# Attention times V on one core: the first unit's load as two halves instead of one transfer

## Chip, cores, metric

One core of one Trainium2 chip. The metric is the device time in microseconds of one execution. "Fast runs" are executions in the chip's normal state.

## The reference

```python
# attn_weights (8, 12, 1024, 1024) float32, v (8, 12, 1024, 64) float32
return np.einsum('bhqs,bhsd->bhqd', attn_weights, v).astype(np.float32)
```

403 MB of attention weights have to be read once and each element is used for 64 products, so the kernel lives from its transfers.

## The kernel before

The work is cut into 48 units. A unit is one load of 128 partitions x 16 rows x 1024, fp32 in memory, cast to bf16 by the DMA, 8 MB read and 4 MB written. Two buffers `abf[0]` and `abf[1]` take the units in turn. PE transposes the 16 rows through four PSUM banks (two bf16 as one fp32 word), VectorE and ScalarE copy each bank out into `at`, PE multiplies with V. The next load into a buffer is issued by GpSimd when the unit in it is transposed. The last two units are loaded in halves, with one semaphore for each second half. (PE is TensorE, the engine for matmuls; a PSUM bank is the buffer that it writes and from which the copies read. A relay by SyncE waits for a load's semaphore and passes it on to PE as `s_half`.)

```python
HALVED = NU - 2                              # NU = 48 units
...
def pe_unit(i, n, loaded, it):
    pe.wait_ge(*loaded)                      # the load (or its first half) has landed
    for g in range(G):                       # 16 rows
        if g == GH:
            pe.wait_ge(s_half, n)            # the second half too: SyncE relays it
        transpose_g(abf[i], g, n)            # g >= 4 waits for the copy of row g - 4
    ...                                      # spread V, transpose back, multiply
...
# VectorE, in program order: V first, then the copies of every unit
nc.vector.wait_ge(s_v0, 16 * 4)
nc.vector.tensor_copy(out=vr..., in_=v32).then_inc(s_vr, 2)
engine(True)
...
# GpSimd
load_attn(0)
load_attn(1)
...
for n in range(NU - 2):
    ...
    pool.wait_ge(s_t[True], (n + 1) * PER_DVE)   # unit n is transposed
    load_attn(n + 2)
    ...                                          # bursts of output stores
...
# SyncE: V's first part by four transfers, then the relays to s_half, then the last stores
```

Of the kernel before, what the change touches and what calls it, by code (L numbers as in the profile page):

```python
# [10 lines left out]
def kernel(  # L11
# [29 lines left out]
    G = Q // VP // 2  # L41
    GH = G // 2
# [5 lines left out]
    NU = 2 * NV  # L48
# [7 lines left out]
    RING = 5  # L56
    NO = 2 * RING

    HALVED = NU - 2

    def slot(q):
        return q % NO
# [20 lines left out]
    with tc.tile_critical(no_gpsimd_drain=True):  # L83
        sem = tc.alloc_semaphore
# [15 lines left out]


        s_abf = [sem(f"s_abf{i}") for i in range(2)]
        s_second = {n: sem(f"s_second{n}") for n in range(HALVED, NU)}
        s_v0, s_v = sem("s_v0"), sem("s_v")
        s_osb, s_held, s_end = sem("s_osb"), sem("s_held"), sem("s_end")

# [13 lines left out]
        s_half, s_free = sem("s_half"), sem("s_free")  # L120
# [193 lines left out]
        pool = nc.gpsimd  # L314

        def load_attn(n):
            pieces = [(0, G)] if n < HALVED else [(0, GH), (GH, GH)]
            for g0, gn in pieces:
                pool.dma_start(  # L319
                    out=abf[n % 2][:, ds(g0, gn)].rearrange("p g s -> p (g s)"),  # L320
                    in_=attn_q[n // 2][:, ds((n % 2 * G + g0) * S, gn * S)],
                ).then_inc(s_abf[n % 2] if g0 == 0 else s_second[n], 16)
# [6 lines left out]
        def store(q, fours, eng, done):  # L329
# [6 lines left out]
            ).then_inc(done, 16)  # L336

        load_attn(0)
        load_attn(1)
        pool.wait_ge(s_memset, 2)  # L340
        pool.affine_select(
# [20 lines left out]
        for n in range(NU - 2):  # L362
            q, i = n // 2, n % 2
            if i == 0 and q % 2 == 1 and q + 1 < NV:
                for s in s_sp:
                    pool.wait_ge(s, 2 * q + 2)
                load_v((q + 1) // 2)
            pool.wait_ge(s_t[True], (n + 1) * PER_DVE)
            load_attn(n + 2)
            if i == 0 and q % BURST == 0 and 0 < q <= HELD_FROM:  # L370
                for k in range(q - BURST, q, 2):
                    store(k, 2, pool, s_osb)
            if i == 1 and q % BURST == 1 and 1 < q:

                pool.wait_ge(s_osb, 16 * (q // 2))
                pool.sem_inc(s_free, BURST // 2)
# [15 lines left out]
        def relay(to, of, n, by=1):  # L392
            nc.sync.wait_ge(of, n)
            nc.sync.sem_inc(to, by)


        for i in range(2):
            relay(s_half, s_abf[i], 16)
        with nc.Fori(1, NV // 2, 1, engines=(mybir.EngineType.SP,)) as it:

            four, eight = (nc.sync.snap(it * x) for x in (32, 16))
            for n in range(4):
                relay(s_half, s_abf[n % 2], four + 16 * (n // 2))
                if n == 2:
                    relay(s_vr, s_v, eight, 2)
        for n in range(HALVED, NU):
            relay(s_half, s_second[n], 16)
        store(NV - 4, 2, nc.sync, s_end)
        store(NV - 2, 1, nc.sync, s_end)
# [41 lines left out]
```

## Time and profile before

| | before |
|---|---|
| time, median of 5 runs of the first comparison | 1054.11 us (1053.88 to 1054.51) |
| span in the profile | 1052.7 us |
| share of GpSimd's DMA queue | 99.0% |
| PE starts unit 0, unit 1 | 28.50, 50.97 us |
| VectorE casts V | 32.72 us |
| GpSimd issues load 2, load 3 | 43.50, 59.29 us |

Read it as a chain. V lands, VectorE is free to copy banks, unit 0 is transposed, buffer 0 is free, load 2 is issued. The lines are in the prediction.

### The profile page before, as it was taken

Reading aid. Unit: us, or ns where it says so; the run is one execution under the profiler, and the core shown is the slowest. Engines: PE = TensorE matmul, PEld = TensorE weight load, DVE = VectorE, ACT = ScalarE, POOL = GpSimd, SP = SyncE. Lnnn points to the kernel's source line nnn. Section 1 sums busy time; section 2 is a strip of 40 time slices with the busy share of each in tenths; the row PEclk is TensorE's granted clock in tenths of the full one; section 3 lists DMA queues with packets and bytes.
Section 4 is the critical chain, followed back from the end, with each engine's and each line's share of the span. In section 5 each row is a group of like instructions: output and inputs, shape, how many; then the busy total and the mean of one; then the engine's idle time right before and its main releaser. Section 6 shows DMA issues by size and latency. Waiting matters only on the chain.

```text
span 1052.7 us, 16580 instructions
## 1 busy us (share of the span) xinstructions
PE 723.3 (69%) x6920; PEld 677.5 (64%) x6920; DVE 388.3 (37%) x582; ACT 410.0 (39%) x493; POOL 44.9 (4%) x80
## 2 busy tenths in 40 slices
PE   0787678578578576467857758668716865875885
PEld 0686577568468565456856758668616865865875
DVE  0443344335335233233523424335303433532543
ACT  0344345335335343233534435335303533533543
POOL 1000000000000010000000000001000000000000
PEclk9989789789799798689979879879857987988998
DMA  9999999999999999999999999999999999999998
GB/s 236 222 217 216 213 214 217 219 219 219 219 217 215 208 218 377 219 219 218 215 217 209 218 218 219 209 230 217 369 214 218 218 210 227 219 207 227 210 215 339
DMA packets 14329, 240.18 MB, mean 228 GB/s; under 512 B 1269, under 2 KB 1781, under 8 KB 4725
## 3 DMA queue, kind: packets, MB, share of 16 engines
q0 software_dynamic: 12912, 233.84, 99.0%
q1 hardware_dynamic: 1413, 6.29, 1.5%
q8 instruction: 2, 0.03, 0.0%
q14 instruction: 2, 0.02, 0.0%
HBM read 427.82 MB, written 25.17 MB: 430 GB/s over the span
## 4 chain that ended last, share of the span: by engine, by line
DMA 70%; PE 23%; issue 5%; another core or an unknown queue 1%; POOL 0%; DVE 0%; SPq 0%; ACT 0%; DVEq 0%; POOLq 0%
DMA abf<-in_attn_weights_dram 68%; PE bank L130 20%; DMA osb<-in_v_dram 3%; PE bank L172 1%; PE bank L145 1%; PE bank L157 0%; POOL vr L325 0%; DVE vbf L230 0%; SPq L387 0%; POOL abf L319 0%; DVE at L251 0%; DVE osb L237 0%; ACT ot L263 0%; DVEq L250 0%
## 5 line engine op out<-in xcount | busy, mean ns | idle before, releaser
L130 PE MATMUL bank<-ident,abf 128*128 128x128 f32 x3072 | 439.5, 312 | 287.7 <-DMA abf<-in_attn_weights_dram 280.4
L130 PEld LDWEIGHTS bank<-ident,abf 128*128 128x128 f32 x3072 | 429.6, 214 | 300.9 <-DMA abf<-in_attn_weights_dram 292.2
L251 DVE COPY at<-bank 128x1024 bf16<-128x1024 bf16 x480 | 319.9, 689 | 464.1 <-PE bank L130 461.8
L251 ACT COPY at<-bank 128x1024 bf16<-128x1024 bf16 x288 | 288.5, 1013 | 419.8 <-PE bank L130 419.8
L172 PE MATMUL bank<-at,vbf 128*64 128x256 bf16 x3072 | 215.0, 278 | 0.0
L172 PEld LDWEIGHTS bank<-at,vbf 128*64 128x64 bf16 x3072 | 196.8, 108 | 13.3 <-DVE at L251 4.0
L263 ACT COPY ot<-bank 128x512 f32<-128x512 f32 x48 | 28.1, 586 | 174.2 <-PE bank L172 174.2
L263 DVE COPY ot<-bank 128x512 f32<-128x512 f32 x48 | 33.2, 692 | 151.3 <-PE bank L172 151.3
L157 PE MATMUL bank<-ident,ot 128*128 128x128 f32 x392 | 52.2, 276 | 33.0 <-DVE vbf L230 32.2
L157 PEld LDWEIGHTS bank<-ident,ot 128*128 128x128 f32 x392 | 43.4, 141 | 45.0 <-DVE vbf L230 44.0
L237 ACT COPY osb<-bank 128x512 f32 (+1 forms) x97 | 52.2, 589 | 27.1 <-PE bank L157 26.3
L319 POOL DMA_DIRECT2D abf<-in_attn_weights_dram x50 | 27.1, 543 | 714.9 <-PE bank L130 713.8
L230 DVE CAST vbf<-bank 128x512 bf16<-128x512 f32 x48 | 30.9, 686 | 6.6 <-PE bank L145 6.6
L230 ACT CAST vbf<-bank 128x512 bf16<-128x512 f32 x48 | 25.8, 589 | 11.8 <-PE bank L145 11.8
L145 PE MATMUL bank<-vr,spread 32*128 32x512 bf16 x384 | 25.7, 377 | 0.0
L325 POOL DMA_DIRECT2D vr<-in_v_dram x11 | 7.8, 705 | 239.2 <-PE bank L145 239.2
L251 ACT ACT_TABLE_LOAD x12 | 15.4, 1283 | 1.3 <-SPq L83 1.1
L145 PEld LDWEIGHTS bank<-vr,spread 32*128 32x128 bf16 x384 | 9.9, 92 | 6.9
L309 DVE CAST vr<-osb 128x4096 bf16<-128x4096 f32 x1 | 2.3, 2295 | 30.1 <-DMA osb<-in_v_dram 30.1
L332 POOL DMA_DIRECT2D out_dram<-osb x10 | 7.1, 716 | 3.4 <-ACT osb L237 3.4
L353 POOL TENSOR_SCALAR_AFFINE_SELECT spread<-spread 32x512 bf16<-32x512 bf16 x4 | 2.5, 632 | 0.6
L237 DVE COPY osb<-bank 128x512 f32<-128x512 f32 x1 | 0.7, 693 | 3.1 <-PE bank L157 3.1
(8 smaller groups left out, 2.1 us busy)
## 6 DMA issues: line engine op xcount, KB each, us to landing
abf<-in_attn_weights_dram POOLq DMA_DIRECT2D x46, 4096.0 KB, 31.2
out_dram<-osb POOLq DMA_DIRECT2D x10, 2048.0 KB, 39.1
vr<-in_v_dram POOLq DMA_DIRECT2D x11, 1024.0 KB, 12.8
abf<-in_attn_weights_dram POOLq DMA_DIRECT2D x4, 2048.0 KB, 24.3
out_dram<-osb SPq DMA_DIRECT2D x1, 2048.0 KB, 14.2
osb<-in_v_dram SPq DMA_DIRECT2D x1, 1024.0 KB
out_dram<-osb SPq DMA_DIRECT2D x1, 1024.0 KB, 16.0
osb<-in_v_dram SPq DMA_DIRECT2D x1, 768.0 KB
```

What stands on the lines that cost most here:

```text
L130: last = pe.matmul(out=pt[g % 4][:, k], lhsT=words[:, k], rhs=ident, is_transpose=True, start=(k == 0), stop=(k == KW - 1),)
L145: last = pe.matmul(out=ps, lhsT=spread[rows, b], rhs=vr[rows, two, b], start=(b == 0), stop=(b == VB - 1),)
L157: last = pe.matmul(out=ps[:, ds(j * P, P)], lhsT=ot[:, j0 + j], rhs=ident, is_transpose=True, start=(j == 0), stop=(j == jn - 1),)
L172: last = pe.matmul(out=outs, lhsT=vbf[:, 2 * kw + par, h], rhs=at[:, ds(half * GH, GH), kw, ds(h * VP, VP), par], start=(n == 0), stop=(n ...
L230: copy(out=vbf[:, :, h], in_=ps.rearrange("p (k d) -> p k d", k=SB)).then_inc(s_vbf[e])
L237: return copy(out=rows.rearrange("p (half j) d -> p j half d", half=2)[:, ds(j0, jn)], in_=ps[:, ds(0, jn * P)].rearrange("p (j half d) -> ...
L251: ins = copy(out=at[:, g].rearrange("c k j two -> c (k j two)"), in_=bank[g % 4].bitcast(bf16),)
L263: copy(out=ot.rearrange("c j (h p) -> c h j p", h=VH)[:, ds(2 * e, 2)], in_=po[e].rearrange("c (h j p) -> c h j p", h=2, j=GH),).then_inc( ...
L319: pool.dma_start(out=abf[n % 2][:, ds(g0, gn)].rearrange("p g s -> p (g s)"), in_=attn_q[n // 2][:, ds((n % 2 * G + g0) * S, gn * S)],).th ...
L325: pool.dma_start(out=vr.rearrange("p two b x -> p two (b x)"), in_=v_2[iv]).then_inc(s_v, 16)
L332: eng.dma_start(out=out_2[q // 2] if fours == 2 else out_q[q], in_=at_slot if fours == 2 else at_slot[:, 0], **({"single_packet": True} if ...
L353: pool.affine_select(out=spread[ds(h * VP, VP)], in_=spread[ds(h * VP, VP)], compare_op=mybir.AluOpType.not_equal, fill=1.0, base=0, patte ...
```

## The change

The intent is to let PE start on the first eight rows while the other eight are still on their way.

```diff
-    HALVED = NU - 2
+    HALVED = (0, NU - 2, NU - 1)
...
-        s_second = {n: sem(f"s_second{n}") for n in range(HALVED, NU)}
+        s_second = {n: sem(f"s_second{n}") for n in HALVED}
...
-            pieces = [(0, G)] if n < HALVED else [(0, GH), (GH, GH)]
+            pieces = [(0, GH), (GH, GH)] if n in HALVED else [(0, G)]
...
-        for i in range(2):
-            relay(s_half, s_abf[i], 16)
+        relay(s_half, s_second[0], 16)
+        relay(s_half, s_abf[1], 16)
...
-        for n in range(HALVED, NU):
+        for n in HALVED[1:]:
             relay(s_half, s_second[n], 16)
```

## The prediction

> **What bounds the kernel now.** I read the page first, then windows of the start and the end, then the chain of waits and the timeline of the first 60 us, and last the trace's single transfer packets. The page:
>
> ```profile
> span 1052.7 us, 16580 instructions
> PE 723.3 (69%) x6920; PEld 677.5 (64%) x6920; DVE 388.3 (37%) x582; ACT 410.0 (39%) x493; POOL 44.9 (4%) x80
> ...
> DMA  9999999999999999999999999999999999999998
> ...
> q0 software_dynamic: 12912, 233.84, 99.0%
> ...
> L319 POOL DMA_DIRECT2D abf<-in_attn_weights_dram x50 | 27.1, 543 | 714.9 <-PE bank L130 713.8
> ```
>
> The sixteen DMA engines are above 90% in 39 of 40 slices, and the queue that GpSimd fills holds them for 99.0% of the span. No compute engine is above 69%. So the bound is the transfer of the attention weights: 48 units of 4 MB as written (bf16), 8 MB as read (fp32). The 715 us that GpSimd waits ahead of its loads (last line) look alarming and are not a loss: it waits for a buffer while an earlier load is still moving.
>
> What matters then is whether the DMA engines ever have nothing to do. The windows over the start and one from the end (columns: stretch and its length; busy time and count for PE, PEld, DVE, ACT, POOL; PE clock, DMA share, GB/s written):
>
> ```profile
> 0.00:2.00 2.00, 0.00 (x0) 0.00 (x0) 0.89 (x3) 0.94 (x1) 0.72 (x5) 1.00 0.10 12
> 2.00:6.00 4.00, 0.00 (x0) 0.00 (x0) 0.52 (x2) 0.34 (x1) 3.31 (x7) 1.00 1.19 399
> 6.00:28.00 22.00, 0.00 (x0) 0.00 (x0) 0.00 (x0) 0.00 (x0) 0.23 (x1) 1.00 1.02 235
> 28.00:44.00 16.00, 12.02 (x80) 11.04 (x80) 8.84 (x11) 6.03 (x6) 0.50 (x1) 0.89 0.95 206
> 44.00:60.00 16.00, 14.66 (x150) 13.81 (x147) 8.61 (x13) 9.11 (x12) 0.60 (x2) 1.00 1.03 220
> ...
> 1000.00:1020.00 20.00, 16.63 (x158) 15.18 (x157) 9.82 (x15) 9.78 (x12) 2.48 (x4) 0.91 1.02 217
> ```
>
> From 2 us on the share stays near 1. (A packet is credited whole near its start and lasts 2.43 us, so windows of a few us scatter by several per cent and no hole can be read from 0.95.) The start is not idle while PE waits 28.5 us: from 2 to 6 us the first value matrix moves (399 GB/s, fp32 to fp32), then attention.
>
> The timeline of the start, filtered to the lines that matter:
>
> ```profile
> 1.48 1.24 POOL L319 DMA_DIRECT2D abf<-in_attn_weights_dram  x2 [1.04 <-SPq L83]
> ...
> 28.50 3.69 PE L130 MATMUL bank<-ident,abf 128*128 128x128 f32 x16 [28.50 <-DMA abf<-in_attn_weights_dram]
> ...
> 32.72 2.29 DVE L309 CAST vr<-osb 128x4096 bf16<-128x4096 f32 x1 [30.15 <-DMA osb<-in_v_dram]
> ...
> 35.67 7.53 PE L130 MATMUL bank<-ident,abf 128*128 128x128 f32 x48 [3.49 <-DVE at L251]
> ...
> 43.50 0.57 POOL L319 DMA_DIRECT2D abf<-in_attn_weights_dram  x1 [37.27 <-PE bank L130]
> ...
> 50.97 8.02 PE L130 MATMUL bank<-ident,abf 128*128 128x128 f32 x64
> ...
> 59.29 0.53 POOL L319 DMA_DIRECT2D abf<-in_attn_weights_dram  x1 [15.22 <-PE bank L130]
> ```
>
> Loads 0 and 1 are issued at 1.5 us. Load 0 lands at 28.2, PE transposes 4 of 16 rows (16 matmuls) and stops: there are four PSUM banks, and the first is copied out by VectorE, which stands in order behind the cast of v, and v lands only at 32.7. So unit 0's transposes end at 43.2, and load 2, which reuses buffer 0, is issued at 43.50. By then load 1 is nearly through. In the packet records (times shifted to the span's start, good to 0.1 us) the sixteen completion writes of load 1 fall between 45.9 and 47.5 us, and several engines then idle until their first packet of load 2: one 1.05 us, others 0.87, 0.74, 0.45, 0.28, 0.18, 0.16, 0.13, the rest under 0.13. Summed over the busy time, 5.0 engine-us are missing between 45.8 and 48.8 (packets in flight 13.7, 13.8 and 15.8 in the three bins of 1 us, against 16.1 in steady flow), that is 0.31 us per engine. After 60 us I find no later hole: load 2, for instance, still has some 9 us to go when load 3 is issued at 59.29 (its unit starts on PE at 68.57).
>
> **What the Trainium skill says.** "DMA: Bandwidth & Descriptors", section "Where 436 GB/s comes from", gives 435 GB/s as the ceiling of the sixteen ports. The trace agrees if the read side is counted: a packet of 32 KB written is 64 KB read in 2.432 us, 26.9 GB/s per engine, 431 for sixteen. Nothing remains to win in steady flow. Same page, "Queues, rings and completion order": an engine takes its queues in turn, one packet at a time. The trace agrees: behind 6 us the last 8 KB packets of v (0.309 us each) come one per attention packet of 2.43 us, and that is why 0.9 MB of v needs until 32.7 us. Same page, "Why a DMA increments its semaphore by 16 and not by 1": each engine posts its own write behind its data, so a load lands with its slowest engine; the 1.6 us spread of load 1's completions is that.
>
> **The change part by part.** Load 0 becomes two transfers, rows 0 to 7 and 8 to 15, each with 128 packets of 16 KB in place of 128 of 32 KB. The sequence of instructions differs in one extra GpSimd issue; the other engines' are the same. SyncE's first relay now waits for the second half, PE's wait at the start for the first.
>
> Cost, on the DMA path. The last two units are halved already, so the trace has 16 KB packets: 1.227 us, against 2.432 for 32 KB. Two halves take 2.454, 0.022 more; 8 pairs per engine make 0.18 us, plus one more completion write of 0.02: 0.20 us on each engine. The extra issue is about 0.57 us of GpSimd (1.24 for two), and delays load 1's issue, the identity and the spread matrix by that; the first attention packets show only at some 5.9 us, load 1 isn't needed before 28, the identity not before 18: nothing on the path.
>
> Gain 1, v lands sooner. On the slowest engine I count about 10 attention packets between its first one and the completion of v, 10 x 2.43 + 7 x 0.31 = 26.5 us from 6-8 us on, which ends near the 32.7 seen. With 16 KB packets: 10 x 1.23 + 2.2 = 14.5 us, so v lands at about 21 to 23 us (estimate).
>
> Gain 2, unit 0 is done sooner. First half: 8 x 1.23 + 7 x 0.31 = 12 us, landing at 19 to 20; PE starts there. VectorE's cast (2.29) ends near 24.5. The second half lands where load 0 did, 28.2, plus 0.2 for smaller packets and about 0.5 for v packets that formerly came behind it: near 29. PE has transposed rows 0 to 7 by then; the 32 matmuls of a second half took 5.6 us in the last units (starts at 1011.93 and 1031.31), so unit 0's transposes end near 34.5, not 43.2, and load 2 is issued at about 34.5 instead of 43.5.
>
> What of this reaches the end? Nine us earlier at PE and GpSimd are worth only what the DMA engines stood dry, because every later load queues behind work that is already there. That is the hole at 46 to 48 us: 0.31 us on the mean engine, 0 to 1.05 on single ones. A load lands with its slowest engine; the two engines that ended load 1 last resumed at 47.8 and 47.9 with holes of 0.28 and 0.74, so I take 0.3 to 0.7 for the ones that set the pace. Sum: -0.3 to -0.7 + 0.20 = -0.1 to -0.5; I take -0.3. The end is untouched: the same last two halved loads and the same stores.
>
> **The rivals.** (a) The 9 us at the start pass through to the end, 1045 us. For it: PE starts some 9 us sooner, and the chain that ended last runs through the transposes of unit 0. Against it: the DMA is at 99%, 233.84 MB of that queue have to go through at the measured rate, and the chain is a chain of releases, not of scarce work; the engine that waits 300 us for data gains nothing by having eight rows early. (b) Only the cost is left: the engines that set the pace had no hole (about half had next to none), so the 0.2 us stays, 1054.4. The trace can't exclude it; it is half as likely as the gain. (c) The smaller transfer starts flowing sooner (fewer bytes to describe before the first packet). Packets per half are as many as per whole, and until 6 us v fills the engines at 399 GB/s anyway; at most a few tenths, 1053.7. (d) The earlier load 2 mixes with v or with load 1 and delays unit 1: both are on the one queue in order, so no; unit 1 would start at about 48 us instead of 50.97, bound by its landing. Its next wait is again a landing.
>
> **Range and chances.** 1054.2 - 0.3 = 1053.9 us. The three runs before spread by 0.4 us, and another session may add as much again; with (b) and (c) inside, the range is 1052.7 to 1055.1. Two per cent are 21 us; nothing at the start other than the whole 28.5 us wait of PE is of that size, and DMA cannot be empty for that long in it. So 1% faster, 98% within, 1% slower.
>
> **What would show it right or wrong.** In the profile of the changed kernel: PE's first transposes at 19 to 20 us; the cast of v at 21 to 23 instead of 32.72; a second start of PE near 29 after a relay by SyncE; GpSimd's third load at 33 to 36; unit 1 on PE at 48; packets without the hole near 47 us; unit 2 landing within half a us of 68.5; DMA share still 99.0%. I am wrong in mechanism if v still lands after 28 us (then the queues are not taken packet by packet, or by other sizes), and wrong in size if the span falls by more than 2 us, which would say that the DMA engines had holes that I haven't found, or rises by more than 1 us, which would say that the small packets cost more at the start than in the last two units.

## More of the kernel before

One more line of the page, for later: the chain that ended last, by engine.

```profile
DMA 70%; PE 23%; issue 5%; another core or an unknown queue 1%; POOL 0%; DVE 0%; SPq 0%; ACT 0%; DVEq 0%; POOLq 0%
```

## The result, and the profile after

1054.84 us median of 5 runs (1054.26 to 1054.85) against 1054.11 before: ratio 1.0005, 95% interval 0.999 to 1.0019. The ratio is the mean time of one kernel's fast runs over that of the other's of the same rounds, so not quite the ratio of these medians. It is the same time. (The medians of this first comparison are 0.7 us apart; a second one, below, has no such gap.)

The page of the changed kernel: the queue is as full as before and carries the same bytes in more packets; the chain that ended last has three points less of DMA.

```profile
span 1053.0 us, 16581 instructions
...
q0 software_dynamic: 13056, 233.84, 99.0%
...
DMA 67%; PE 24%; issue 4%; another core or an unknown queue 3%; POOL 1%; DVE 0%; ACT 0%; POOLq 0%; SPq 0%
```

144 packets more is 128 for the halves and 16 completion writes. The shift in the chain shows how little its shares say about time: PE's part changed and the span did not follow.

The timeline of the start, the same lines as in the prediction (start, length, engine, line, operation, idle before and what ended it):

```profile
1.48 1.77 POOL L319 DMA_DIRECT2D abf<-in_attn_weights_dram  x3 [1.04 <-SPq L83]
...
19.40 6.12 PE L130 MATMUL bank<-ident,abf 128*128 128x128 f32 x32 [19.40 <-DMA abf<-in_attn_weights_dram]
20.14 2.29 DVE L309 CAST vr<-osb 128x4096 bf16<-128x4096 f32 x1 [17.57 <-DMA osb<-in_v_dram]
...
28.56 4.11 PE L130 MATMUL bank<-ident,abf 128*128 128x128 f32 x32 [3.05 <-SPq L394]
...
32.97 0.57 POOL L319 DMA_DIRECT2D abf<-in_attn_weights_dram  x1 [26.22 <-PE bank L130]
...
47.85 9.30 PE L130 MATMUL bank<-ident,abf 128*128 128x128 f32 x64 [7.33 <-DMA abf<-in_attn_weights_dram]
...
57.45 0.53 POOL L319 DMA_DIRECT2D abf<-in_attn_weights_dram  x1 [23.91 <-PE bank L130]
```

PE starts 9.1 us sooner, V is cast 12.6 us sooner (20.14 for 32.72), load 2 is issued 10.5 us sooner (32.97 for 43.50) and load 3 1.8 us sooner (57.45 for 59.29). By unit 1 most is gone: 47.85 for 50.97, because unit 1 has to land, and the queue brings it when it brings it. The windows say the same (stretch and length; busy time and count of PE, PEld, DVE, ACT, POOL; PE clock, DMA share, GB/s written):

```profile
2.00:6.00 4.00, 0.00 (x0) 0.00 (x0) 0.51 (x2) 0.34 (x1) 3.42 (x7) 1.00 1.00 330
6.00:28.00 22.00, 6.12 (x32) 5.53 (x32) 5.47 (x6) 3.04 (x3) 0.63 (x1) 1.00 1.07 241
28.00:44.00 16.00, 10.61 (x120) 9.28 (x120) 5.34 (x8) 5.72 (x8) 0.57 (x1) 1.00 0.98 212
44.00:60.00 16.00, 12.15 (x102) 11.93 (x104) 6.63 (x10) 7.09 (x8) 0.53 (x1) 0.79 1.05 226
```

From 6 to 28 us PE did 6 us of work where it did none before; the transfer rate in the same stretch is 241 against 235 GB/s.

The trace's single packets give the finer picture. A whole load is 128 packets of 32 KB, eight on each of the sixteen DMA engines, and sixteen completion writes, one per engine. Between the completion of load 1 and that of load 2 the mean engine needs 19.94 us before and 19.39 after; a whole load in steady flow, later in the same traces, needs 19.32. So the hole, the time in which engines stood still for want of load 2, is gone, and the mean engine gained 0.55 us. Of the 0.61 us over the steady flow, 0.29 were standing still, 0.20 packets that took longer, and 0.12 two instruction fetches that fell into this load.

Which engine a packet ran on is not recorded, but the packets of one engine can be chained: each data packet starts 0.019 us before the one ahead of it ends, and the next load's first packet starts 0.021 us after the completion write. In the kernel before, thirteen engines went from load 1 to load 2 so, without a gap. Only the three that had ended load 1 first (at 45.63, 45.72 and 45.81 us) stood still; they resumed at 46.65, 47.56 and 47.70, 4.7 us together. (Times from the span's start; the prediction's packet times are 0.3 us larger.) In the changed kernel no engine has a gap there.

At the end of the last load the mean engine is still 0.16 us ahead (1029.24 against 1029.40). The span is 0.3 us longer all the same.

### The profile page after: what moved, and what is told of

It reads as the page before. It is cut to its first block, busy times and chain, and to the rows that moved or that the text cites. A ratio compares the mean times of both kernels' runs of the same rounds, so it can differ in the third digit from the quotient of the medians.

```text
span 1053.0 us, 16581 instructions
## 1 busy us (share of the span) xinstructions
PE 726.8 (69%) x6920; PEld 680.8 (65%) x6920; DVE 387.9 (37%) x582; ACT 410.1 (39%) x493; POOL 45.3 (4%) x81
## 4 chain that ended last, share of the span: by engine, by line
DMA 67%; PE 24%; issue 4%; another core or an unknown queue 3%; POOL 1%; DVE 0%; ACT 0%; POOLq 0%; SPq 0%
DMA abf<-in_attn_weights_dram 67%; PE bank L130 22%; PE bank L172 1%; PE bank L145 1%; POOL vr L325 1%; PE bank L157 0%; POOL abf L319 0%; DVE vbf L230 0%; DVE osb L237 0%; ACT ot L263 0%; POOLq L366 0%; SPq L394 0%; POOLq L446 0%; POOLq L376 0%
## 5 line engine op out<-in xcount | busy, mean ns | idle before, releaser
L157 PE MATMUL bank<-ident,ot 128*128 128x128 f32 x392 | 52.2, 276 | 33.0 <-DVE vbf L230 32.2
```

Source lines behind the costliest of these rows:

```text
L157: last = pe.matmul(out=ps[:, ds(j * P, P)], lhsT=ot[:, j0 + j], rhs=ident, is_transpose=True, start=(j == 0), stop=(j == jn - 1),)
```

## Experiments

I had two questions: is it true that only the hole counts, and why does the filled hole not show? For the second I had found, in the packet records, that during the three bursts of output stores one engine falls behind: in the kernel before, relative to the earliest engine, it stands at 0.335 us, after the first burst at 1.028, after the second at 1.708, after the third at 3.087 (which engine is the same one across a burst is inferred: the other offsets stay within 4 ns, and in the last burst two engines move). Theory L says that this engine ends the kernel and had no hole. Theory N says that there is nothing to explain below 0.5 us.

All kernels gave correct results. Times are medians, with the kernel before of the same rounds beside them.

### The two kernels again

No edit.

> The kernel before, unchanged, timed against itself: what the method calls a difference when there is none, and a second profile of the same program. Every theory: ratio 1.000, difference of means under 0.3 us. In its profile I look for the one engine that falls behind in the bursts of output stores (theory L: one DMA engine ends the kernel, it falls behind by 0.3 to 1.4 us in each burst of stores, and it had no hole near 47 us): L expects it again, with the last completion write of the kernel 1.2 to 1.6 us behind the middle engine's. Rival N (the 0.5 us between the two kernels is chance of one run or profile): this pair differs by as much as 0.5 us too, and the straggler is not there or is another size.

> The changed kernel again. Theory L (the engine that ends the kernel had no hole, so it keeps only the cost of 0.2 us for the smaller packets and about 0.1 for a later start): +0.2 to +0.5 us against the kernel before, as in the first result. Rival N (chance): between -0.3 and +0.1. Theory of the prediction (hole filled on the engines that set the pace): -0.1 to -0.5.

Measured: the kernel before against itself 1054.85 to 1055.00 (ratio 0.9999, 0.9986 to 1.0013); the changed kernel 1054.67 to 1055.00 (0.9999, 0.9986 to 1.0013). N was right about the time: the gap of the first comparison did not come back, and 0.3 us cannot be told in either direction. L's +0.2 to +0.5 did not show, but an interval of 1.4 us either way does not exclude it. What L says of the trace held: the straggler is there in both profiles and completes GpSimd's last store at 1046.50 and 1046.97 us, as at 1046.54 and 1047.12 in the first two.

### Load 2 held back by the same wait in both kernels

```diff
+            if n == 0:
+                for s in s_m:
+                    pool.wait_ge(s, 1)       # unit 0's products
             load_attn(n + 2)
```

> The kernel before, with load 2 held back until unit 0's products are done: issue at about 51.1 us instead of 43.5. Bound by the DMA engines (my theory): load 1 has left the engines at 45.6 to 47.3 us, load 2's packets come 3.3 us after its issue, at 54.4, so every engine stands still for some 7.1 to 8 us, and all of it reaches the end: 1054.1 + 7.3 = 1061.4, from 1060.8 to 1062.2. Rival S (what counts at the start is when PE and the other engines get their first work, and small delays of a load are taken up by the 9 us of slack of the later loads): PE's first two units start when they did, so 1054 to 1056.

> The changed kernel with the same added wait: issue at about 40.6 us instead of 33.0, first packets at 43.9, before load 1 has left the engines (46.2 at the earliest). My theory: no hole, the time of the changed kernel, 1054.3 to 1054.9; the 10 us that the change gave at the start are slack, and this wait eats 7.6 us of it for nothing. Rival S: the same loss as the same wait costs in the kernel before.

Measured: in the kernel before 1059.40 (1059.29 to 1061.47) against 1055.00, ratio 1.0049 (1.0033 to 1.0064); in the changed kernel 1054.61 against 1055.00, ratio 0.9997 (0.9981 to 1.0012). One wait, 4.4 us in one kernel and nothing measurable in the other. Rival S is out: PE's first two units began at 29.20 and 49.07 us (28.50 and 50.97 in the kernel before), and the time was lost. Windows of the two, first the kernel before with the wait:

```profile
44.00:48.00 4.00, 4.00 (x59) 3.75 (x58) 0.69 (x1) 1.07 (x2) 0.00 (x0) 1.00 0.44 94
46.00:51.00 5.00, 5.00 (x66) 4.72 (x61) 1.56 (x3) 1.25 (x2) 0.57 (x1) 1.00 0.06 10
```

and the issue of its load 2 in the timeline:

```profile
49.71 0.57 POOL L319 DMA_DIRECT2D abf<-in_attn_weights_dram  x1 [43.49 <-PE bank L172]
```

Then the windows of the changed kernel with the wait:

```profile
44.00:48.00 4.00, 0.16 (x1) 0.16 (x2) 0.00 (x0) 0.00 (x0) 0.00 (x0) 0.51 1.11 238
46.00:51.00 5.00, 3.16 (x15) 3.16 (x16) 0.98 (x2) 1.01 (x1) 0.00 (x0) 0.51 1.04 223
```

and the same issue there:

```profile
41.06 0.58 POOL L319 DMA_DIRECT2D abf<-in_attn_weights_dram  x1 [34.30 <-PE bank L172]
```

In the first, PE is busy all the time and the DMA engines move 10 GB/s: that is what a real loss looks like here, and it is the picture opposite to the one that made PE's wait at the start look costly. In the second, PE is busy for 0.16 of the first 4 us, and the DMA is full. The size of my expectation was off (7.3 for 4.4): V landed 1.8 us sooner in that execution, so the issue came at 49.71, not 51.1, and the first packets followed 1.3 to 2.3 us after the issue, not 3.3. Worked out with what was measured, it fits: load 1 to load 2 took 24.42 us on the mean engine, 4.3 to 4.5 more than in the two profiles of the kernel before (19.94, 20.08), and the time rose by 4.4.

### PE late, with halves

```diff
         pe.wait_ge(s_const, 1 + VH)
+        pe.wait_ge(s_half, 1)                # both halves of unit 0, before anything
```

> The changed kernel, but PE waits for both halves of unit 0 before its first transpose: starts at 28.5 us instead of 19.3, unit 0's transposes end near 37.5 and load 2 is issued there. My theory (only the time at which the DMA engines run dry counts, 45.6 us): no hole, same time as the changed kernel and as the kernel before, 1054.3 to 1055.0, although PE begins 9 us later. Rival S (PE's early start is what counts): up to 9 us more.

Measured: 1054.75 against 1054.74, ratio 1.0001 (0.9988 to 1.0015). PE starts at 28.80 us, load 2 goes out at 39.47, and there is no hole (19.41 us from load 1 to load 2):

```profile
28.80 10.38 PE L130 MATMUL bank<-ident,abf 128*128 128x128 f32 x64 [28.80 <-SPq L395]
...
39.47 0.57 POOL L320 DMA_DIRECT2D abf<-in_attn_weights_dram  x1 [32.73 <-PE bank L130]
```

The part of the change that its intent names, PE's early start, is worth nothing measurable; in this variant it is V's early landing alone that brings load 2 out in time.

### The hole closed with whole loads

```diff
-        nc.vector.wait_ge(s_v0, 16 * 4)
-        nc.vector.tensor_copy(out=vr..., in_=v32).then_inc(s_vr, 2)
...
+        pool.wait_ge(s_const, 1 + VH)
+        pool.wait_ge(s_v0, 16 * 4)
+        pool.tensor_copy(out=vr..., in_=v32).then_inc(s_vr, 2)
         for n in range(NU - 2):
```

> The kernel before with whole loads, but the first cast of v moved from VectorE to GpSimd, so that VectorE copies unit 0's banks from 28.5 us on instead of 35. Unit 0's transposes should end near 38 us; GpSimd's cast (estimate 5 us, from 0.63 us for 512 elements a partition in its affine selects) ends near 37.5; load 2 goes out at about 38 instead of 43.5. The hole near 47 us is closed at no cost in packets. The mean engine's load 2 should land 0.5 us sooner than in the kernel before. Theory of the prediction (the hole reaches the end): -0.3 to -0.6 us. Theory L (the engine that ends the kernel had no hole): 0 +- 0.2. If GpSimd's cast takes over 8 us, the hole stays and the run says nothing.

Measured: 1054.95 against 1054.74, ratio 1.0002 (0.9989 to 1.0016). The timeline shows that the edit did its work:

```profile
28.70 9.13 PE L130 MATMUL bank<-ident,abf 128*128 128x128 f32 x64 [28.70 <-DMA abf<-in_attn_weights_dram]
...
30.94 3.60 POOL L362 CAST vr<-osb 128x4096 bf16<-128x4096 f32 x1 [24.73 <-DMA osb<-in_v_dram]
38.13 0.57 POOL L317 DMA_DIRECT2D abf<-in_attn_weights_dram  x1 [3.59 <-PE bank L130]
```

Unit 0 is transposed in one go, load 2 leaves at 38.13, the mean engine needs 19.41 us from load 1 to load 2 and ends the last load at 1029.09, 0.3 to 0.4 us ahead of the kernel before. The time is not measurably shorter; the interval, 1.2 us down to 1.7 us up, is wider than the 0.3 to 0.6 at stake. So the time alone does not decide between the theories. The packet records do, in the next part, and in this kernel load 0 has no small packets that could hide a gain.

### Which engine ends the kernel

No run of its own; this table reads the packet records of ten profiles, three of them of the runs in the next part. "Straggler" is the engine that falls behind in the bursts: its completion of the same load before the first burst; it is the one that the first burst sets back by 0.67 to 0.69 us (in six of the ten profiles the burst moves one or two other engines too, by about 0.2 us at most). All times are in us from the trace's first instruction, which is the span's start.

| kernel | load 2 issued | load 1 to load 2, mean engine | last load done, mean engine | straggler before the bursts | SyncE's last store done, last engine |
|---|---|---|---|---|---|
| before | 43.50 | 19.94 | 1029.40 | 192.11 | 1050.69 |
| before_again | 43.77 | 20.08 | 1029.53 | 192.10 | 1050.66 |
| after | 32.97 | 19.39 | 1029.24 | 192.43 | 1050.99 |
| after_again | 34.34 | 19.41 | 1029.24 | 192.28 | 1050.83 |
| after_load2_late | 41.06 | 19.41 | 1029.21 | 192.32 | 1050.90 |
| after_pe_late | 39.47 | 19.41 | 1029.16 | 192.02 | 1050.60 |
| before_pool_cast | 38.13 | 19.41 | 1029.09 | 192.27 | 1050.86 |
| before_many_packets | 41.67 | 19.46 | 1029.01 | 192.00 | 1050.57 |
| after_many_packets | 33.10 | 19.40 | 1029.20 | 192.59 | 1051.15 |
| pool_cast_many_packets | 38.75 | 19.40 | 1029.05 | 192.08 | 1050.67 |

The last two columns differ by 858.55 to 858.59 us, taken with three decimals, in every row. Where that one engine stands 192 us into the kernel decides, to 0.05 us, when the last store is done, and the span ends 2.0 us after that; where the mean engine stands does not. Nor does the issue of the last stores: they leave SyncE at 1044.22 us in the first row and at 1042.39 in the second, and are done at 1050.69 and 1050.66. The two profiles with the hole (first two rows) have this engine at 192.10 and 192.11, the eight without it at 192.00 to 192.59: filling the hole does not move it forward. The hole was on others: followed packet by packet through load 2, the three engines that stood still in the kernel before are 0.92, 0.99 and 2.17 us behind the earliest one at 192 us, the straggler 0.33; in before_again five engines stood still (one for 0.06 us only), and the straggler is again not among them. What spreads its position by 0.6 us from profile to profile is open.

Three profiles are not in the table. In before_load2_late all sixteen engines stood still; one candidate for the straggler there stands at 197.01, 4.9 us later than in the kernel before, and the last store is done at 1055.58, also 4.9 us later. (The first burst moves many engines in that run, so the candidate is picked by the fit.) all_halved and none_halved have other transfers after 192 us; their differences are 859.97 and 858.86.

The row before_many_packets shows one thing more. It has the start of the kernel before, and hardly a hole: V had landed at 30.5 us in that execution, 1.8 us sooner than in the first two rows (32.3 and 32.2), and load 2 left at 41.67. The flag plays no part before the first store, so the kernel before probably has the hole in some of its executions only.

### Is it the packet flag of the stores?

```diff
-                **({"single_packet": True} if eng is pool else {}),
```

taken from the kernel before, from the changed one, and from the one with the cast on GpSimd.

> The kernel before without the single-packet flag on GpSimd's output stores, to see whether that flag is what puts one DMA engine behind. So far that engine loses 0.69, 0.68 and about 1.3 us in the three bursts of stores, in each of six profiles that I compared, and completes GpSimd's last store at 1046.5 to 1047.1 us. Theory L1 (one packet of a whole row blocks that engine): without the flag its last completion falls to 1044 to 1045, the kernel ends up to 1 us sooner, 1053.8 to 1054.5. Rival L2 (the flag is innocent, that engine is slower for stores that GpSimd describes): same growth, 1054.7. A third way: more, smaller turns between the queues disturb the loads, 1055 or more.

> The changed kernel without that flag. L1: straggler gone, then the mean engine counts, and the 0.3 us by which its loads land sooner in the changed kernel should show: 0.2 to 0.4 under the kernel before without the flag. L2: as the changed kernel, 1054.5 to 1055.0, and no difference to the kernel before without the flag.

> The cast on GpSimd and no single-packet flag: hole closed, whole loads, and under L1 no straggler. If any of these versions beats both kernels, it is this one. L1: 1053.5 to 1054.3. L2: 1054.7 to 1055.0.

Measured, against 1054.60: 1054.40 (ratio 0.9997, 0.9983 to 1.0010), 1054.87 (1.0001, 0.9987 to 1.0014), 1054.73 (1.0000, 0.9987 to 1.0014). Rival L2: the flag is innocent. The straggler is there without it, with the same steps (0.69 and 0.68 us in the first two bursts), and GpSimd's last store completes on it at 1046.71, 1047.29 and 1046.80 us. None of the three beats the kernel before by more than the noise. Why this engine is slower at stores stays open.

### What one halving costs, and what it is worth at the end

```diff
-    HALVED = (0, NU - 2, NU - 1)
+    HALVED = tuple(range(NU))                # second halves on s_second[n % 2]
```

> Every unit loaded in halves, 45 more than in the changed kernel. Two sizes for the cost of one halving are at stake. The prediction's step (two packets of 1.227 us for one of 2.432, eight times, and one more completion write: 0.20 us): 45 x 0.20 = 9.0, so 1063.6 against 1054.8 before. From the completion writes of the last two units (a half every 9.686 us, a whole every 19.323; packets overlap a little): 0.05 us each, so 45 x 0.05 = 2.2 and 1057.0. A rival that nobody pays for it because PE starts each unit half a load sooner: 1054.8 or less.

Measured: 1056.40 against 1054.74, ratio 1.0014 (0.9999 to 1.0029). That is 1.7 us for 46 halvings more than the kernel before has, some 0.04 us each; the interval, up to 3.1 us, allows 0.07 and excludes the prediction's 0.20. The packet records agree: the mean engine ends the last load at 1031.38, 2.2 us after the changed kernels of the table (1029.21 on average), which is 0.05 for each of 45 halvings.

```diff
-    HALVED = NU - 2
+    HALVED = NU                              # none; relays wait for the whole load
```

> No unit in halves, not even the last two. If a half landing early is worth something where nothing queues behind it, the end shows it: PE starts the last unit's second half of 32 matmuls (5.6 us) after the last landing; with a whole load it starts 64 matmuls (about 10 us), so the last output store is issued about 4.4 us later, at 1048.6 instead of 1044.2, a little before the stores ahead of it are through (1049.5): the end 1 to 3 us later, 1055.8 to 1057.8 against 1054.8. Rival: the DMA engines are the only bound, also at the end, and the kernel gains 0.1 for two halvings less: 1054.7.

Measured: 1055.29 against 1054.74, ratio 1.0004 (0.9989 to 1.0019): about half a us; the interval, 1.2 us down to 2.0 us up, excludes the upper half of the 1 to 3 expected, not the lower. The end is cushioned too. The timeline of the end shows SyncE's last stores at 1047.54 us

```profile
1032.26 7.95 PE L130 MATMUL bank<-ident,abf 128*128 128x128 f32 x64 [1.39 <-DMA abf<-in_attn_weights_dram]
...
1047.54 0.93 SPq L417 DMA_DIRECT2D out_dram<-osb  x2
```

instead of 1044.22: 3.3 us later, less than 4.4 because PE ran this last unit in 7.95 us, and most of that passes while earlier stores are still draining. The span in the profile is 1053.6, 0.9 longer; but 0.7 of that the straggler has already at 192 us (192.79 for 192.11), which leaves 0.2 to 0.3 us for the end.

## Why the prediction was right, point by point

**The bound.** Right. All 99% is transfer, and the two runs with the same added wait show it in both directions: 4.4 us when it empties the queue, nothing measurable when it does not. The 431 GB/s of the prediction is a little small, as packet records overlap: with one packet every 2.413 us it is 435. That this is the ceiling which the prediction cites is not shown: the page's figure is for the ports of SBUF, and only the half that is written, 217 GB/s, goes there.

**V lands sooner because queues alternate by packet.** The mechanism is right: between 9 and 12 us the records have 16 packets of V and 16 of attention in the kernel before, 32 and 32 in the changed one. VectorE's cast begins at 20.14, 0.9 us before the 21 to 23 said.

**Unit 0 and load 2.** Right: PE at 19.40 (19 to 20), its second start after a relay by SyncE at 28.56 (near 29), unit 1 at 47.85 (48). Load 2 at 32.97 is 1.5 us sooner than the 34.5 said, as the second half's 32 matmuls took 4.11 us, at a granted clock of 1.00, and not the 5.6 read at the kernel's end, where it was 0.70. In after_again they took 5.44 at 0.71, and load 2 went out at 34.34.

**The hole.** That load 2 comes too late for some engines was right, and so was the idle sum (4.7 engine-us for the 5.0 said). Where it lay was read wrong: not eight engines with gaps of 0.13 to 1.05 us, but the three that had ended load 1 first, with 0.8 to 2.0 us each. Packets also took longer around it (up to 3.58 us for 2.43), twelve of load 2's sixteen first packets, nine of them on engines that had not stood still.

**The cost of halving.** 0.20 us of the sum, from two packets of 1.227 against one of 2.432. Each record overlaps the next by 0.019 us, so durations must not be added; completion to completion a halved unit takes 9.686 twice against 19.323, that is 0.05, and the run with every unit halved says 0.04 to 0.05. All the same, the changed kernel pays about 0.15 us on the mean engine: in the table its five profiles end the last load at 1029.16 to 1029.24, the three with whole loads and no hole at 1029.01 to 1029.09. So the 0.20 came out near by luck; what the other 0.1 is, no run separates.

**From engines to the end.** This step failed: "the two engines that ended load 1 last resumed at 47.8 and 47.9 with holes of 0.28 and 0.74, so I take 0.3 to 0.7 for the ones that set the pace." The two engines that ended load 1 last (47.08 and 47.26) went on to load 2 after 0.02 us; the late resumptions belong to engines that had ended it first. And the engines that are last at 47 us are not the one that is last at 1050. That one falls behind in the bursts of stores, had no hole, and stands on average no earlier without the hole than with it (192.25 against 192.10 us in the table). So the term is 0 by the traces, the sum is about the cost alone, and rival (b), "the engines that set the pace had no hole", comes nearest. The number, 1053.9 for 1054.84, held because all terms are tenths of a us and the comparison, good to 1 to 2 us, can't tell them apart: it is luck, and no support for the sum. Unit 2 landed 1.3 us sooner on PE (67.26 for 68.57), more than the half us said. In the kernel before, the engine that ended load 2 last (68.21; eight data packets per engine settle its chain) was one of the three with the hole; it also drew the 3.58 us packet and an instruction fetch of 0.94 us. It then stays the last engine in every load to the end, so for PE's start of unit 2 the hole did count; the kernel's end does not follow it.

## What to carry to other kernels

When one resource is busy 99% of the time, count an early start elsewhere only by the time for which that resource would otherwise have stood dry; test it by adding the same delay to both versions, for the one that has slack won't feel it. A filled hole counts at the end only if it was on the engine that finishes last: follow that engine back from the end instead of taking the one that is last at the hole, and chain packets by their exact times before saying which engine stood still. And take the cost of a transfer from completion to completion, not from the sum of packet durations.

## What the Trainium skill lacked or had wrong

- "DMA: Bandwidth & Descriptors", section "Latency and other measured facts", says that engines 7 and 15 are usually slower than the others. Here one engine (the records don't number them) lost 0.69 and 0.68 us in two bursts of stores that GpSimd issued, while its offset from the others stayed within 4 ns through 200 us of loads ahead of them. The page does not say that such a lag may come from stores alone, or that it decides the end.
- The same section gives about 1 us from issue to the first byte on GpSimd's path. Measured from the start of the issue to the first packets: 1.3 to 2.3 us with all engines empty (before_load2_late), 3.2 to 4.2 on the three empty engines of the kernel before while the others were at work, and 4.1 for the first load of the kernel, beside V's packets.
- No page says that the packets around an empty stretch run longer: 2.5 to 3.5 us instead of 2.43, on all sixteen engines in before_load2_late.
- No page gives the cost of halving packets of this size: 16 KB against 32 KB written, 0.05 us per 4 MB in the records, 0.04 in the time (interval 0 to 0.07).
- No page that I read says what an instruction fetch costs a running load: two packets of 16 KB on the instruction queue took 0.94 and 0.97 us of one engine each, at 52.6 and 60.8 us in the kernel before.
